# Twelve of the gate tiles of the first half computed in six pairs, seven products for eight, with PSUM banks read in the middle of their sums

## The chip, the cores and the metric

The kernel runs on one core of a Trainium2 chip. The metric is device time in microseconds (us), the median of three runs. Engines are named as the profile names them: PE is TensorE, PEld its weight loads, DVE is VectorE, ACT is ScalarE, POOL is GpSimd, and SP is SyncE, which here issues every DMA, one after the other in the order of its queue.

## The reference

One layer of a decoder on a sequence of 2048 tokens (and 16 meta tokens ahead of them), 1024 features wide, in float32. All projections come from one matrix of 1024 x 6400:

```python
xn = rms_norm(h, norm_gain[l])
proj = xn @ w_in[l]
sb_q, sb_k, sb_v, sw_q, sw_k, sw_v, sb_z, sw_z, g_sb, g_sw = jnp.split(proj, offsets, axis=-1)
o_sb = stick_breaking_attention(sb_q, sb_k, sb_v, valid)            # 8 heads, full length
o_sw = sliding_window_sink_attention(rope(sw_q), rope(sw_k), sw_v)  # 16 heads, window 128
y_sb = (o_sb * jax.nn.silu(sb_z)) @ w_branch_sb[l]
y_sw = (o_sw * jax.nn.silu(sw_z)) @ w_branch_swa[l]
merged = jax.nn.sigmoid(g_sb) * y_sb + jax.nn.sigmoid(g_sw) * y_sw
h = h + merged @ w_out[l]
return rms_norm(h, final_norm_gain)
```

(Reshapes and masks are left out.) The last four parts of the projection, `sb_z` (512 columns), `sw_z`, `g_sb` and `g_sw` (1024 each), are the gates: 28 tiles of 128 columns. They need nothing of the attention, so the kernel can compute them at any point where TensorE has room.

## The kernel before

**Tiles.** The sequence is cut into four groups of 512 columns. Groups 2 and 3 are the first half and are worked through from the projection to the two attentions; groups 0 and 1 are the second half. Features lie on the partitions, in eight slices of 128 (`k`). To keep float32 accuracy each matrix is split into a high and a low part of a type that TensorE multiplies at full rate (fp32r), and a product of such matrices is three matmuls: high by high, high by low, low by high. One tile of the projection (128 columns of `w_in` against one group) is therefore 8 x 3 = 24 matmuls into one PSUM bank, written by `gemm` (lines 409, 410, 411). A gate tile is done by `gate`: 24 matmuls for each of the two groups of the half, a sigmoid on ACT that reads the bank (L577), for `sw_z` and `sb_z` a multiplication on DVE (L579), and a store of 256 KB to DRAM.

**Weights.** `weights` serves one column tile. In the first half it loads the raw 512 KB into one of two `raw` buffers, splits it (`wh` by a copy, L108, `wl` by a subtraction, L109; on POOL while the flags `hsplit` and `vsplit` are False, on ACT and DVE when they are True), and stores both parts to DRAM. In the second half it loads the two stored parts (two times 512 KB). `wh` and `wl` have three buffers each.

**The stick-breaking attention** (`stick`) runs in rows: a product of keys and queries (L876), a sigmoid on ACT (L879), for the diagonal blocks a mask on POOL (L881), a scan along the row on DVE (L883), four transposes on PE (L896), the split of their result on ACT (L112) and DVE (L113), and the product with the values (L927). TensorE works on a row's transposes some five rows after its L876 (`LT`). The first half has 96 rows, 64 of them with the mask; the second has 224. DVE is the busiest of the engines that a row needs, so `weave` puts the k steps of gate tiles between the rows, at a ratio that spreads the rows over the gate tiles given to it: tiles 4 to 24 in the first half (`rest = 25`), 4 to 22 in the second. Tiles 0 to 3 come earlier. In the first half a row also carries, in 16 of the cases, the squares of the input of the second half (`xq`, L860), whose sums the normalization of that half needs; `xq` shares two buffers with the queries `q`.

**Between the halves.** After the last row of the first half, three gate tiles are left. `by_group` computes all three for group 2 and the first for group 3; then `prep` normalizes and splits the input of group 0 into the buffers of group 2 (a row `rb` from ACT, L374; then for each of eight slices a load `xs`, L382 on DVE, L383 on ACT, L385 on DVE), while TensorE does the two gate tiles left for group 3.

**Order.** The order on TensorE is written out by hand; that of DVE, ACT, POOL and SP in this part is set by the scheduler of the program from its estimates, and each engine works strictly in the order given to it.

## Time and profile before

| what | value |
|---|---|
| median of three runs | 2133.44 us (2133.14 to 2135.09) |
| profiled execution: time, span | 2136.89 us, 2135.0 us |
| PE busy, matmul records | 2112.2 us, 10534 |
| DVE, ACT, POOL busy | 1383.4, 1030.5, 333.1 us |
| DMA moved | 380.39 MB, 178 GB/s over the span |
| stretch of the stick-breaking rows, first half | about 395 to 738 us |
| the same, second half | about 1138 to 1627 us |

A row of the timeline gives start, duration, engine, line, operation, output and inputs, and in brackets how long the engine stood idle before it and what released it. Matmuls overlap, so the time that one costs is the distance between starts and not its duration. Of a table by stretches the columns are the busy time of PE, PEld, DVE, ACT and POOL with the count of instructions, then the granted clock, the share of the DMA engines and GB/s.

### The profile page before, as it was taken

The numbers are of one execution on the slowest core, as the hardware profiler recorded it, in microseconds if no ns is written. First come the engines' busy times: TensorE is split into PE (matmuls) and PEld (weight loads), VectorE is DVE, ScalarE is ACT, GpSimd is POOL, SyncE is SP. The second block draws the span as 40 slices with busy tenths as digits, with TensorE's granted clock in tenths as the row PEclk, the third lists the DMA queues.
The fourth block names the chain that finished last, engine by engine and source line by source line (L and its number), as shares of the span: only waits on it lengthen the run. The fifth ranks groups of instructions, "written<-read, shape, count | busy, mean of one in ns | idle before, by whom it ended". The sixth has DMA issues, their size and how long they took to land.

```text
span 2135.0 us, 30157 instructions
## 1 busy us (share of the span) xinstructions
PE 2112.2 (99%) x10534; PEld 1755.9 (82%) x10534; DVE 1383.4 (65%) x2158; ACT 1030.5 (48%) x2471; POOL 333.1 (16%) x453
## 2 busy tenths in 40 slices
PE   8999999999999999999999999999999999999998
PEld 6788888888888788888888888888888888887887
DVE  7797885466555443867746888888885446553453
ACT  6677774344444434777744565555554202221121
POOL 2122332332232300122210000000000232000000
PEclk9999999999999999999999999999999999999999
DMA  9855455766556464443465333323423986557432
GB/s 334 289 182 194 173 177 175 233 219 208 183 184 204 151 221 159 157 157 139 138 196 165 121 123 118 120 97 112 119 85 132 346 297 198 192 216 270 157 110 79
DMA packets 174519, 380.39 MB, mean 178 GB/s; under 512 B 22720, under 2 KB 40960, under 8 KB 174368
## 3 DMA queue, kind: packets, MB, share of 16 engines
q1 hardware_dynamic: 174368, 378.48, 52.5%
q8 instruction: 83, 1.36, 0.3%
q14 instruction: 68, 0.56, 0.1%
HBM read 237.35 MB, written 140.98 MB: 177 GB/s over the span
## 4 chain that ended last, share of the span: by engine, by line
PE 85%; issue 7%; DMA 3%; DVE 2%; ACT 1%; SPq 1%; POOL 0%; POOLq 0%; DVEq 0%; ACTq 0%
PE ps_g L409 15%; PE ps_g L411 14%; PE ps_g L410 14%; PE ps_o L927 5%; PE ps_t L896 4%; PE ps_z L876 4%; PE ps_z L718 3%; PE ps_o L764 3%; PE ps_g L232 1%; PE ps_g L233 1%; PE ps_z L231 1%; PE ps_z L233 1%; PE ps_z L232 1%; PE ps_g L231 1%; PE ps_t L747 1%
## 5 line engine op out<-in xcount | busy, mean ns | idle before, releaser
L409 PE MATMUL ps_g<-xh,wh 128*128 128x512 f32 x1544 | 634.6, 411 | 7.0 <-ACT xh L979 7.0
L410 PE MATMUL ps_g<-xl,wh 128*128 128x512 f32 x1544 | 605.9, 392 | 0.0
L411 PE MATMUL ps_g<-xh,wl 128*128 128x512 f32 x1544 | 605.9, 392 | 0.0
L883 DVE TENSOR_TENSOR_SCAN row<-row 128x512 f32<-128x512 f32 (+2 forms) x320 | 375.6, 1175 | 157.9 <-POOL row L881 105.8
L411 PEld LDWEIGHTS ps_g<-xh,wl 128*128 128x128 f32 x1544 | 290.2, 188 | 65.5 <-DVE wl L109 0.3
L409 PEld LDWEIGHTS ps_g<-xh,wh 128*128 128x128 f32 x1544 | 291.3, 189 | 52.7 <-ACT xh L979 7.0
L410 PEld LDWEIGHTS ps_g<-xl,wh 128*128 128x128 f32 x1544 | 292.0, 189 | 43.2 <-DVE xl L980 1.3
L879 ACT ACTIVATE row<-ps_z 128x512 f32<-128x512 f32 (+2 forms) x320 | 165.0, 516 | 192.0 <-PE ps_z L876 191.3
L113 DVE SCALAR_TENSOR_TENSOR wtl<-ps_t,wth 128x512 fp32r<-128x512 f32 (+1 forms) x320 | 189.9, 594 | 55.7 <-ACT wth L112 54.9
L112 ACT ACTIVATE wth<-ps_t 128x512 fp32r<-128x512 f32 (+1 forms) x320 | 170.5, 533 | 71.8 <-PE ps_t L896 68.9
L876 PE MATMUL ps_z<-kt,q 128*128 128x512 f32 (+4 forms) x640 | 178.2, 353 | 0.0
L896 PE MATMUL ps_t<-ident,row 128*128 128x128 f32 x1088 | 171.1, 272 | 1.9 <-DVE wtl L113 1.2
L896 PEld LDWEIGHTS ps_t<-ident,row 128*128 128x128 f32 x1088 | 135.7, 140 | 39.1 <-DVE wtl L113 2.3
L881 POOL TENSOR_SCALAR_AFFINE_SELECT row<-row 128x128 f32<-128x128 f32 x128 | 42.0, 329 | 630.1 <-ACT row L879 591.0
L876 PEld LDWEIGHTS ps_z<-kt,q 128*128 128x128 f32 x640 | 118.9, 188 | 23.2
L927 PE MATMUL ps_o<-wth,vc 128*128 128x512 f32 (+1 forms) x320 | 125.1, 391 | 0.0
L108 POOL TENSOR_SCALAR wh<-raw 128x1024 fp32r<-128x1024 f32 (+1 forms) x63 | 68.2, 1082 | 336.1 <-PE ps_g L410 209.5
L726 ACT ACTIVATE sc<-sc,nm 128x129 f32<-128x129 f32 x256 | 100.2, 394 | 41.7 <-DVE nm L724 40.9
L927 PE MATMUL ps_o<-wtl,vc 128*128 128x512 f32 (+1 forms) x320 | 116.9, 365 | 0.7 <-DVE wtl L113 0.7
L577 ACT ACTIVATE tmp<-ps_g 128x512 f32<-128x512 f32 x112 | 67.0, 599 | 103.9 <-PE ps_g L411 97.5
L109 POOL TENSOR_TENSOR wl<-raw,wh 128x1024 fp32r<-128x1024 f32 (+1 forms) x43 | 100.5, 2337 | 3.3
L270 ACT CAST ringl<-gt 128x512 fp32r<-128x512 f32 x32 | 20.0, 624 | 152.3 <-DVE gt L268 144.6
(316 smaller groups left out, 3439.2 us busy)
## 6 DMA issues: line engine op xcount, KB each, us to landing
wh<-h_in_w_in SPq DMA_DIRECT2D x66, 512.0 KB, 3.6
wl<-l_in_w_in SPq DMA_DIRECT2D x66, 512.0 KB, 4.9
raw<-in_w_in SPq DMA_DIRECT2D x50, 512.0 KB, 5.1
h_in_w_in<-wh SPq DMA_DIRECT2D x50, 512.0 KB, 2.9
l_in_w_in<-wl SPq DMA_DIRECT2D x50, 512.0 KB, 2.9
q<-qd SPq DMA_DIRECT2D x128, 128.0 KB, 3.1
vc<-vd SPq DMA_DIRECT2D x48, 256.0 KB, 3.3
kd<-tmp SPq DMA_DIRECT2D x32, 256.0 KB, 3.9
```

What stands on the lines that cost most here:

```text
L109: (V if vsplit[0] else G).tensor_tensor(l, src, f32(h), op=ALU.subtract)
L112: A.activation(h, acc, AF.Copy, scale=scale)
L113: V.scalar_tensor_tensor(l, acc, scale, f32(h), op0=ALU.mult, op1=ALU.subtract)
L409: T.matmul(acc, lhsT=wh[:, k, :], rhs=xh[g][:, k, :], start=k == 0, stop=False)
L410: T.matmul(acc, lhsT=wh[:, k, :], rhs=xl[g][:, k, :], start=False, stop=False)
L411: T.matmul(acc, lhsT=wl[:, k, :], rhs=xh[g][:, k, :], start=False, stop=k == KT - 1)
L726: A.activation(sc[:, hh, :], sc[:, hh, :], AF.Exp, bias=nm[:, hh:hh + 1], accum_out=den[:, hh:hh + 1])
L876: T.matmul(acc[:, :b - a], lhsT=lq, rhs=kt[h][:, k0 + a:k0 + b], start=t == 0, stop=t == 1)
L879: A.activation(r[:, a:b], acc[:, :b - a], AF.Sigmoid, scale=-1.0)
L883: V.tensor_tensor_scan(r[:, :w], r[:, :w], r[:, :w], last[j] if n else 1.0, op0=ALU.mult, op1=ALU.min)
L896: T.transpose(tr[:, j * P:(j + 1) * P], rows_of[h, g, n - (j > i), j][:, k0:k0 + P], ident)
L927: T.matmul(o[:, :n], lhsT=v, rhs=r, start=first and r is wh, stop=last and r is wl)
```

## The change

Gate tiles are regrouped. The list of 28 is now `sb_z` (4), `g_sb` (8), four of `g_sw`, `sw_z` (8), the other four of `g_sw`. In the first half only tiles 4 to 11 (the eight of `g_sb`) are woven into the stick-breaking rows (`REST[0] = 12`; the ratio goes from 0.60 to 1.58, the second half's stays 1.515). After the rows come three tiles of `g_sw` (12, 13, 14) the usual way, their weights split on ACT and DVE, and then tiles 16 to 27 as six pairs. Tile 15 is computed for group 2 ahead of `prep` and for group 3 behind it.

A pair is a product of a 2 x 2 block matrix of weights (two column tiles by two halves of the features) with a 2 x 2 block matrix of inputs (two halves of the features by two groups). It is done in Winograd's form of Strassen's scheme: seven block products of 4 x 3 = 12 matmuls each, 84 for a pair where two tiles for two groups took 96. The blocks are sums of blocks. `sums_of_x` makes those of the input once, in four steps of 12 DVE operations and four ACT copies; the first three steps stand ahead of the three usual tiles on the other engines, as far as the scheduler leaves them there. `pair_weights` makes those of the weights for each pair: it loads two raw tiles into the two `raw` buffers, and DVE and ACT form sums and high and low parts. `seven` does the products in three PSUM banks: two banks are read when a part of their sum is in and are then added to further (`start=False`). Since `KEEP_PAIRS` is False, the split weights of these twelve tiles are not stored; in the second half `weights` finds no stored parts for them and loads the raw tile, splits it on POOL, and stores the parts, which nobody reads. Seven of those tiles lie among the woven ones of the second half, five behind them.

```diff
+REST = (12, 23)
+KEEP_PAIRS = False
...
+    def sums_of_x(bp, groups):
...
+        for k in range(KT // 2):
+            yield q
+            b11, b12, b22 = (whole(n, k) for n in ("11", "12", "22"))
+            V.tensor_tensor(b11, b12, b11, op=ALU.subtract)
+            V.tensor_tensor(b12, b22, b12, op=ALU.subtract)
+            V.tensor_tensor(b22, b22, b11, op=ALU.subtract)
+            halves_of("t2", k, b22)
+            halves_of("t3", k, b12)
+            halves_of("t1", k, b11)
+            b21 = whole("21", k)
+            V.tensor_tensor(b21, b21, b22, op=ALU.subtract)
+            halves_of("t4", k, b21)
+        yield q
+
+    def pair_weights(bp, ca, cb):
...
+            a, b = load(ca), load(cb)
...
+            def parts(hl, t):
+                A.copy(hl[0], t)
+                V.tensor_tensor(hl[1], t, f32(hl[0]), op=ALU.subtract)
+            parts(t1, a)
+            V.tensor_tensor(s[:, hi], a[:, lo], b[:, lo], op=ALU.subtract)
+            V.tensor_tensor(b[:, lo], b[:, lo], b[:, hi], op=ALU.add)
+            V.tensor_tensor(s[:, lo], b[:, lo], a[:, lo], op=ALU.subtract)
+            parts(t3, s)
+            parts(t2, b)
+            V.tensor_tensor(s4, a[:, hi], s[:, lo], op=ALU.subtract)
+            parts(t4, s4)
...
+    def seven(w, b, tags, use):
...
+        a0, a1, a2 = (ps(t) for t in tags)
+        p1, u2, u3 = tmp(), tmp(), tmp()
+        product(a0, "11", "11", True, False)
+        A.copy(p1, a0)
+        product(a1, "s2", "t2", True, False)
+        V.tensor_tensor(u2, a1, p1, op=ALU.add)
+        product(a0, "12", "21", False, True)
+        use(0, 0, a0)
+        product(a1, "s3", "t3", False, False)
+        V.tensor_tensor(u3, a1, p1, op=ALU.add)
+        product(a2, "s1", "t1", True, False)
+        V.tensor_tensor(u3, a2, u3, op=ALU.add)
+        use(1, 1, u3)
+        product(a1, "22", "t4", False, True)
+        V.tensor_tensor(p1, a1, p1, op=ALU.add)
+        use(1, 0, p1)
+        product(a2, "s4", "22", False, True)
+        V.tensor_tensor(u2, a2, u2, op=ALU.add)
+        use(0, 1, u2)
...
-            rest = 25 if half == 0 else 23
+            rest = REST[half]
...
-            ts = [mk() for mk in gts[rest:]]
-            drain(by_group(ts, groups[:1]), by_group(ts[:1], groups[1:]))
+            with tc.tile_pool(name="pairs", bufs=1, side="left") as bp:
+                hsplit[0] = vsplit[0] = True
+                ts = [mk() for mk in gts[rest:15]]
+                hsplit[0] = vsplit[0] = False
+                sums_q = sums_of_x(bp, groups)
+                tq = [next(sums_q) for _ in range(3)][0]
+                for n, t in enumerate(ts):
+                    if n == 1:
+                        next(sums_q)
+                    drain(by_group([t], groups))
+                pairs = [gate_pair(bp, gss[n], gss[n + 1], groups, tq) for n in range(16, 28, 2)]
+                next(pairs[0])
+                next(sums_q)
+                drain(*pairs)
+            ts = [gts[15]()]
+            drain(by_group(ts, groups[:1]))
             prep(halves[1][0], rs0)
-            drain(by_group(ts[1:], groups[1:]))
+            drain(by_group(ts, groups[1:]))
```

Lines of the changed kernel stand two lower than before up to the new functions (L55 becomes L57, L579 becomes L581), and 114 lower behind them (L876 becomes L990). In the rows below a name's number is that of the tile, and the brackets name the engines or DMA queues whose semaphores the instruction waits for.

**The hand-over to the pairs, on DVE.** Before, the last split of the rows (`wtl`) and the reciprocal root for the next half's normalization are followed at once by `prep`:

```order
L113 SCALAR_TENSOR_TENSOR wtl_8261<-ps_t_8255,wth_8260 128x512 [waits Activation_49]
L117 TENSOR_SCALAR sum_8279<-sum_8279 128x8 [waits DVE_49]
L932 TENSOR_TENSOR xs_7610<-tmp_8274 64x512 [waits Activation_49]
L123 TENSOR_TENSOR sum_8280<-rs_8283 128x8 [waits DVE_49,PE_49,Activation_49]
L934 TENSOR_TENSOR xs_7610<-tmp_8270,xs_7610 128x512
L124 TENSOR_TENSOR sum_8280<-sum_8280,sum_8279 128x8 [waits DVE_49]
L125 TENSOR_SCALAR sum_8280<-sum_8280 128x8 [waits DVE_49]
L126 TENSOR_TENSOR rs_8283<-rs_8283,sum_8280 128x8 [waits DVE_49]
L382 SCALAR_TENSOR_TENSOR xs_8443<-xs_8443,gn_67,rb_8436 128x512 [waits DMAHW3_49,Activation_49]
L382 SCALAR_TENSOR_TENSOR xs_8448<-xs_8448,gn_67,rb_8436 128x512 [waits DMAHW7_49,DMAHW0_49]
```

Now the sums of the input and of the weights of the first pairs stand in between. Below is the stretch about the last of them: `wl_7692` is the low part of the sum t2 of pair 0, `t3l`, `t2l` are slices of the input sums, and `s_7857<-raw_7853,raw_7855` (L636) is the first sum of pair 1, whose raw tiles are loaded at that point.

```order
L634 TENSOR_TENSOR wl_7692<-raw_7697,wh_7691 128x1024 [waits DMAHW5_49,PE_49,Activation_49]
L634 TENSOR_TENSOR s4l_7694<-tmp_7700,s4h_7693 128x512 [waits Activation_49]
L606 TENSOR_TENSOR tmp_7713<-tmp_7715,tmp_7713 128x512 [waits DVE_49]
L607 TENSOR_TENSOR tmp_7715<-tmp_7717,tmp_7715 128x512 [waits DVE_49]
L601 TENSOR_TENSOR t1l_7456<-tmp_7713,t1h_7455 128x512 [waits Activation_49]
L608 TENSOR_TENSOR tmp_7717<-tmp_7717,tmp_7713 128x512 [waits DVE_49]
L636 TENSOR_TENSOR s_7857<-raw_7853,raw_7855 128x512 [waits DMAHW6_49,DMAHW0_49]
L601 TENSOR_TENSOR t3l_7454<-tmp_7715,t3h_7453 128x512 [waits Activation_49]
L613 TENSOR_TENSOR tmp_7728<-tmp_7728,tmp_7717 128x512 [waits DVE_49]
L637 TENSOR_TENSOR raw_7855<-raw_7855 128x512 [waits DVE_49]
L601 TENSOR_TENSOR t2l_7452<-tmp_7717,t2h_7451 128x512 [waits Activation_49]
```

The last slices of `t3l` and `t2l`, which pair 0 reads, stand behind L636 of pair 1 on the same engine.

**In a pair, on DVE and SP.** Before, the leftover tiles need nothing of DVE, and SP carries their stores and, from row `wh_8542` on, the loads for the next half:

```order
L55 DMA gw5_2_229<-tmp_8347 128x512 [waits DMAHW4_49,Activation_49]
L55 DMA gw6_2_233<-tmp_8375 128x512 [waits DMAHW5_49,Activation_49]
L55 DMA gw7_2_237<-tmp_8403 128x512 [waits Activation_49]
L55 DMA wh_8542<-h_in_w_in_512_318 128x1024 [waits DMAHW7_49,PE_49]
L55 DMA wl_8543<-l_in_w_in_512_319 128x1024 [waits DMAHW0_49,PE_49]
L55 DMA gw5_3_230<-tmp_8431 128x512 [waits DMAHW1_49,Activation_49]
```

Now DVE does this about the boundary of pairs 0 and 1 (L680 is the last addition for pair 0, L641 its neighbour for the weights s4 of pair 1, L636 and L637 are the first sums of pair 2, and L668 reads pair 1's bank z when its second product is in):

```order
L680 TENSOR_TENSOR tmp_7737<-ps_t_7735,tmp_7737 128x512 [waits PE_49]
L641 TENSOR_TENSOR tmp_7858<-raw_7853,s_7857 128x512 [waits DMAHW1_49]
L691 TENSOR_TENSOR tmp_7841<-tmp_7737,tmp_7841 128x512 [waits Activation_49]
L634 TENSOR_TENSOR s4l_7852<-tmp_7858,s4h_7851 128x512 [waits Activation_49]
L636 TENSOR_TENSOR s_7995<-raw_7991,raw_7993 128x512 [waits DMAHW5_49,DMAHW3_49]
L637 TENSOR_TENSOR raw_7993<-raw_7993 128x512 [waits DVE_49]
L668 TENSOR_TENSOR tmp_7875<-ps_z_7872,tmp_7874 128x512 [waits DMAHW2_49,PE_49,Activation_49]
L638 TENSOR_TENSOR s_7995<-raw_7993,raw_7991 128x512 [waits DVE_49]
```

and SP this (`raw_7991` and `raw_7993` are the tiles of pair 2, into the buffers of `raw_7853` and `raw_7855`):

```order
L57 DMA zw0_2_145<-tmp_7777 128x512 [waits DMAHW1_49,DVE_49]
L57 DMA zw1_3_150<-tmp_7807 128x512 [waits DMAHW2_49,DVE_49]
L57 DMA raw_7991<-in_w_in 128x1024 [waits DMAHW3_49,DMAHW0_49,DVE_49]
L57 DMA zw1_2_149<-tmp_7824 128x512 [waits DMAHW4_49,DVE_49]
L57 DMA raw_7993<-in_w_in 128x1024 [waits DMAHW6_49,DMAHW5_49,DVE_49]
L57 DMA zw0_3_146<-tmp_7841 128x512 [waits DVE_49]
```

L668 of pair 1, which TensorE needs before it adds its fourth product to that bank, stands behind the sums of pair 2 and so behind their loads.

**`prep` of group 0, on ACT.** Before, one gate tile's sigmoid (`tmp_8431`) ends ahead of `rb`, and two more (`tmp_8508`, `tmp_8536`) run between the copies of the input slices:

```order
L577 ACTIVATE tmp_8431<-ps_g_8406 128x512 [waits DMAHW1_49,PE_49]
L374 COPY rb_8436<-ps_t_8437 128x512 [waits PE_49]
L383 CAST xh_8434<-xs_8443 128x512 [waits DVE_49]
L383 CAST xh_8434<-xs_8448 128x512 [waits DVE_49]
L383 CAST xh_8434<-xs_8453 128x512 [waits DVE_49]
L383 CAST xh_8434<-xs_8458 128x512 [waits DVE_49]
L577 ACTIVATE tmp_8508<-ps_g_8483 128x512 [waits DMAHW2_49,PE_49]
L383 CAST xh_8434<-xs_8463 128x512 [waits DVE_49]
L383 CAST xh_8434<-xs_8468 128x512 [waits DVE_49]
L383 CAST xh_8434<-xs_8473 128x512 [waits DVE_49]
L577 ACTIVATE tmp_8536<-ps_g_8511 128x512 [waits PE_49,Activation_49]
L383 CAST xh_8434<-xs_8478 128x512 [waits DVE_49]
```

Now it is the only tile's sigmoid for group 3 (`tmp_8634`) that stands between the fourth and the fifth copy, and the next copies are followed by the second half's own:

```order
L579 ACTIVATE tmp_8557<-ps_g_8532 128x512 [waits DMAHW3_49,PE_49,Activation_49]
L376 COPY rb_8562<-ps_t_8563 128x512 [waits PE_49]
L385 CAST xh_8560<-xs_8569 128x512 [waits DVE_49]
L385 CAST xh_8560<-xs_8574 128x512 [waits DVE_49]
L385 CAST xh_8560<-xs_8579 128x512 [waits DVE_49]
L385 CAST xh_8560<-xs_8584 128x512 [waits DVE_49]
L579 ACTIVATE tmp_8634<-ps_g_8609 128x512 [waits DMAHW4_49,PE_49,Activation_49]
L385 CAST xh_8560<-xs_8589 128x512 [waits DVE_49]
L385 CAST xh_8560<-xs_8594 128x512 [waits DVE_49]
L385 CAST xh_8560<-xs_8599 128x512 [waits DVE_49]
L385 CAST xh_8560<-xs_8604 128x512 [waits DVE_49]
```

TensorE has one tile for one group to do behind `rb` there, where before it had two.

61 lines of the change are left out of this document (57 added, 4 removed).

## The prediction

> **What bounds the kernel now.** I read the page first, then a table by stretches, then the waits of TensorE, then the timeline at the places that the change touches.
>
> ```profile
> span 2135.0 us, 30157 instructions
> PE 2112.2 (99%) x10534; PEld 1755.9 (82%) x10534; DVE 1383.4 (65%) x2158; ACT 1030.5 (48%) x2471; POOL 333.1 (16%) x453
> PE 85%; issue 7%; DMA 3%; DVE 2%; ACT 1%; SPq 1%; POOL 0%; POOLq 0%; DVEq 0%; ACTq 0%
> ```
>
> PE is busy for 99% of the span and carries the chain that ends last. So a matmul removed is time gained, unless PE then waits. PE's waits are few now:
>
> ```profile
> PE ps_g L409 <- ACT xh L979: 7.0, 1, 7.0
> PE ps_o L409 <- ACT xh L383: 1.6, 1, 1.6
> PE ps_t L896 <- DVE wtl L113: 1.2, 2, 0.6
> ```
>
> None of these lies at the leftover gate tiles or at `prep` of group 0 (there PE runs on, below). Every new wait is therefore a loss that the kernel does not have now.
>
> ```profile
> 500.00:600.00 100.00, 99.34 (x513) 82.61 (x512) 55.52 (x69) 45.78 (x114) 25.95 (x28) 1.00 0.59 194
> 1300.00:1400.00 100.00, 100.00 (x545) 83.73 (x544) 83.65 (x103) 58.53 (x125) 3.54 (x12) 1.00 0.40 121
> 1700.00:1800.00 100.00, 100.00 (x443) 82.84 (x442) 48.48 (x58) 11.43 (x19) 32.66 (x24) 1.00 0.74 263
> ```
>
> The first row is the woven stretch of the first half: DVE (third pair of columns) 56%, POOL 26%. The second is that of the second half: DVE 84%, and POOL nearly idle, since weights come split; the third, the tail of the second half, is spoken of at the end. The change makes the first stretch as dense as the second, and puts POOL's splits into both.
>
> **What is gained.** Matmuls follow each other at 0.228 us:
>
> ```profile
> 695.11 0.39 PE L409 MATMUL ps_g<-xh,wh 128*128 128x512 f32 x1
> 695.33 0.39 PE L410 MATMUL ps_g<-xl,wh 128*128 128x512 f32 x1
> 695.56 0.40 PE L411 MATMUL ps_g<-xh,wl 128*128 128x512 f32 x1
> ```
>
> Between the starts at 738.25 and 760.03 (both rows below) stand 96, so 0.227 each over whole tiles. Six pairs save 12 matmuls each, 72 in all: 72 x 0.227 = 16.3 us. A product of 12 takes 2.72 us, a pair 19.1 instead of 21.8, a tile for one group (24) 5.45. The other matmuls only move. Now the waits.
>
> **(a) The hand-over into the pairs.** Call T0 the end of the rows:
>
> ```profile
> 738.25 0.39 PE L409 MATMUL ps_g<-xh,wh 128*128 128x512 f32 x1
> ```
>
> Three usual tiles hold PE until T0 + 6 x 5.45 = 32.7. DVE is free of the square root at about T0 + 4 and does 36 operations of the input sums ahead of the pairs. What 512 columns cost:
>
> ```profile
> 1651.92 0.69 DVE L199 TENSOR_TENSOR tmp<-tmp 128x512 f32<-128x512 f32 x1 [0.66 <-DMA tmp<-zw]
> 1652.53 0.68 DVE L203 TENSOR_TENSOR ringl<-tmp,ringl 128x512 fp32r<-128x512 f32 x1
> ```
>
> 0.61 us start to start, so 22 us: hidden under the three tiles. But the third weight sum of pair 0 takes the `wh` and `wl` buffers of the third tile, which PE frees at T0 + 32.7. Then:
>
> ```profile
> L109 DVE TENSOR_TENSOR wl<-raw,wh x22: 1205/1220/1627, 14.3 to 345.7; 128x1024 fp32r<-128x1024 f32 x22
> L106 ACT CAST wh<-raw x2: 1032/1043/1054, 13.2 to 15.4; 128x1024 fp32r<-128x1024 f32 x2
> DMA to landing us min/median/max: 4.2/5.1/8.8
> ```
>
> The cast on ACT (1.04) and the subtraction on DVE (1.22) end at T0 + 35.2; only then is the raw buffer free, and SP issues the second raw tile of pair 1 at about T0 + 35.6. The last row is the landing of raw tiles in the whole trace; 8.8 belongs to the first 50 us, and the one measured in each later stretch took
>
> ```profile
> DMA to landing us min/median/max: 4.2/4.2/4.2
> DMA to landing us min/median/max: 5.1/5.1/5.1
> ```
>
> from 50 to 395 and from 395 to 740 us. On DVE the sum L636 of pair 1 waits for that tile, and the last slices of pair 0's input sums stand behind it: five operations, 3.1 us. They end at T0 + 42.9 to 43.8, and PE asks for the last slice of t2 in its second product, at T0 + 32.7 + 2.72 + 2.04 = 37.5. Wait 5.4 to 6.3, taken 5.8. Without the load DVE's own queue (ten operations) ends at T0 + 41.3, wait 3.8; with 8.8 it is 10.0. After a wait of that size PE may start slowly; the one long wait of the trace ends so:
>
> ```profile
> 7.01 0.79 PE L409 MATMUL ps_g<-xh,wh 128*128 128x512 f32 x1 [7.01 <-ACT xh L979]
> 8.81 0.63 PE L409 MATMUL ps_g<-xh,wh 128*128 128x512 f32 x1
> 11.64 0.39 PE L409 MATMUL ps_g<-xh,wh 128*128 128x512 f32 x1
> ```
>
> Nine matmuls in 4.63 us, 2.6 more than at 0.227, partly for want of input. I take half, 1.3 (0 to 2.6). The Trainium skill, "TensorE: Matmul & The Clock Gate", section "Part 1: The HAM clock gate", has TensorE fall to half its clock when it idled for a window of some 3.4 us, until it was busy about as long again; by that rule the term would be about 1.7 (an estimate from that page). **(a) = 7.1**, 3.8 to 12.6.
>
> **(b) Between pairs.** The raw tiles of pair n+2 can be loaded when DVE has done s4 of pair n+1, behind the last addition of pair n. DVE's read of bank z (L668) in pair n+1 stands behind the two sums of pair n+2, which wait for these loads; PE's fourth product may not start before that read. From the end of pair n: 0.17 release, two operations 0.61 + 0.69, issues 0.85, landing 4.6 (between the two rows above), two sums and the read 2.0: 8.9. PE arrives after three products, 8.2. Late by 0.7, in four of the six pairs: **(b) = 2.8**; at 4.2 us of landing 1.3, at 5.1 it is 4.9, at 8.8 it would be 19.7. The reads in the middle cost no more than this: the copy of the first bank on ACT (0.6 us, as a sigmoid of that shape below) has the second product, 2.72 us, to hide behind; if that cover went, the third product would be late.
>
> **(c) `prep` of group 0.** PE needs the last low slice for the eighth step of the first product of the second half:
>
> ```profile
> 760.03 0.60 PE L368 MATMUL ps_t<-ident,rs 128*128 128x128 f32 x4
> 771.75 0.48 PE L409 MATMUL ps_g<-xh,wh 128*128 128x512 f32 x1
> 776.64 0.39 PE L409 MATMUL ps_g<-xh,wh 128*128 128x512 f32 x1
> ```
>
> ```profile
> 761.34 2.74 DVE L382 SCALAR_TENSOR_TENSOR xs<-xs,gn,rb 128x512 f32<-128x512 f32 x4 [18.91 <-ACT rb L374]
> 771.70 1.41 DVE L382 SCALAR_TENSOR_TENSOR xs<-xs,gn,rb 128x512 f32<-128x512 f32 x2 [1.36 <-DMA xs<-in_xt]
> 774.14 0.69 DVE L385 TENSOR_TENSOR xl<-xs,xh 128x512 fp32r<-128x512 f32 x1 [0.31 <-ACT xh L383]
> ```
>
> Now the slice is there at 774.8 and asked for (L410) at 776.9: 2.1 us to spare. One tile less of cover, 5.5 us, makes it 3.4 late at this pace; without the waits for loads (eight of each at 0.70 and 0.68, 11.0 us from 761.3) it is there at 772.4, 1.0 late. The last two loads again stand behind a weight load on SP, so I stay near the first: **(c) = 2.8**.
>
> **(d) The woven stretches.** Fifteen splits on POOL fall into dense stretches, eight in the first half, seven in the second, where before loads of split weights stood. What one does to DVE:
>
> ```profile
> 507.39 2.32 DVE L883 TENSOR_TENSOR_SCAN row<-row 128x272 f32<-128x272 f32 x1 [0.28 <-ACT row L879]
> 520.49 0.72 DVE L883 TENSOR_TENSOR_SCAN row<-row 128x272 f32<-128x272 f32 x1 [1.34 <-POOL row L881]
> ```
>
> ```profile
> 506.74 2.39 POOL L109 TENSOR_TENSOR wl<-raw,wh 128x1024 fp32r<-128x1024 f32 x1
> ```
>
> The same scan takes 2.32 us instead of 0.72 beside POOL's subtraction, and ends with it. The Trainium skill ("SBUF — State Buffer", section "Who interferes with whom") calls the port pair that DVE shares with GpSimd an exclusive lock; these rows agree. Scans came 3.4 us apart so far, and PE hardly noticed:
>
> ```profile
> L883 DVE TENSOR_TENSOR_SCAN row<-row x96: 448/1224/3319, 398.4 to 724.2; 128x512 f32<-128x512 f32 x32, 128x528 f32<-128x528 f32 x16, 128x400 f32<-128x400 f32 x16, 128x272 f32<-128x272 f32 x16
> ```
>
> With 13 tiles of 10.9 us taken out they come about 2 us apart, as in the second half. There the room is this:
>
> ```profile
> 1301.86 0.60 PE L896 MATMUL ps_t<-ident,row 128*128 128x128 f32 x4
> 1305.52 0.60 PE L896 MATMUL ps_t<-ident,row 128*128 128x128 f32 x4
> ```
>
> ```profile
> 1303.21 0.67 DVE L113 SCALAR_TENSOR_TENSOR wtl<-ps_t,wth 128x512 fp32r<-128x512 f32 x1
> ```
>
> The bank t of the first transposes is read out at 1303.88 and taken again at 1305.52: 1.64 us to spare. A delay of 1.60 just fits; the longest that the trace has,
>
> ```profile
> 1667.85 2.88 DVE L203 TENSOR_TENSOR ringl<-tmp,ringl 128x512 fp32r<-128x512 f32 x1
> ```
>
> against 0.68, with some 0.4 before it, is 2.6, so 1.0 over. Between 0 and 1.0 for each split, I take 0.2, nearer the scan's row since it is the scan that fills DVE there: 15 x 0.2 = 3.0 (0 to 15; a gain is excluded, PE is at 100% there). Next, the squares share buffers with the queries:
>
> ```profile
> DMA to landing us min/median/max: 3.2/4.1/5.0
> DMA to landing us min/median/max: 2.6/3.1/4.8
> L577 ACT ACTIVATE tmp<-ps_g 128x512 f32<-128x512 f32 x112 | 67.0, 599 | 103.9 <-PE ps_g L411 97.5
> ```
>
> `xq` lands in 4.1, is squared in about 0.8, and then `q` in 3.1: 8.0 us, against four rows and their gate steps, about 9.7 (53 matmuls at 0.183, 545 in 100 us). At the upper ends it is 10.6. I take 0.2 for each of seven heads, 1.4 (0 to 7). At the end of the rows a tile's split on DVE (1.22) stands ahead of the last `wtl`: half, 0.6. **(d) = 5.0.**
>
> **Costed at nothing.** In the tail of the second half, five splits on POOL and stores that nobody reads: DVE is at 48% there, POOL has a row of weights ahead of PE, and the stores wait on SP only for POOL. Should POOL be late, the first gate tile of the tail is.
>
> **The sum.** 7.1 + 2.8 + 2.8 + 5.0 = 17.7 lost against 16.3 gained: +1.4 us. The profiled execution (2136.89, span 2135.0) would go to 2138.3; it lies 3.45 above the median 2133.44, so the median goes to **2134.8**, with its own range 2130 to 2139.
>
> **Rivals.** *Loads and splits are covered (faster).* DMA moves little while pairs run (two raw tiles and four stores in 19 us), so landing is at the low end, 4.2 or less, and DVE does not stop PE in the rows. For it: the 84% of DVE in the second half leave PE at 100%. Against: the order on DVE. (a) 3.8, (b) 1.3, (c) 1.5, (d) 0.6: 7.2 lost, 9.1 gained, 2124. *POOL's lock stops the rows (slower).* Place: L113 in both dense stretches, 15 splits. Price: 1.0 each instead of 0.2, +12, so 2147. For it: 2.88 us beside POOL, and masks of the first half queue on POOL behind a split of 3.4 us. Against: DVE idles 16 us in 100 and catches up before the next split, some 25 us later. It decides from 0.4 us for each split. *Raw tiles take 7 us in the pairs (slower).* 2.4 more than taken in four pairs and in (a): +12, 2147; spoken for only by the first 50 us.
>
> **How the numbers follow.** A measurement tells about 0.2% from no change, 4.3 us. Forecast 0.40, covered loads 0.30, lock 0.22, slow loads 0.08. The forecast's range reaches a little over both bounds of 4.3, so faster 0.31, same 0.38, slower 0.31. The range takes in both rivals' centres: 2123 to 2147.
>
> **What would show it.** PE with 72 matmuls less; a wait of some 5.8 us on `t2l` in the first pair; four of under 1 us on L668; one of 2 to 3 us at the first tile of the second half; waits on L113 in the rows that lie just behind a POOL subtraction. The forecast is wrong if the pairs run at 19.1 us each without waits, or if the waits on L113 sum to over 6 us.

## The result: 33 us slower, and where they went

The changed kernel takes 2166.41 us (median of four runs, 2164.77 to 2166.51), the kernel before 2133.29 in the same comparison: ratio 1.0152, 95% interval 1.0135 to 1.017. The prediction was 2134.8 (2123 to 2147). From the page of the changed kernel:

```profile
span 2164.6 us, 30201 instructions
PE 2112.2 (98%) x10462; PEld 1748.4 (81%) x10462; DVE 1466.1 (68%) x2287; ACT 1057.8 (49%) x2520; POOL 328.5 (15%) x447
PE 60%; DVE 4%; DMA 4%; issue 2%; ACT 1%; SPq 0%; POOL 0%; DVEq 0%; POOLq 0%; ACTq 0%
```

72 matmuls are gone, but PE's busy time is the same 2112.2 us, and the span is 29.6 longer. (By the medians it is 33.1; the profiled execution of the kernel before, 2136.89, lies 3.6 above its median.) The list of PE's waits, here down to 1.2 us, shows one part (columns: total us, times, longest); that of before had 7.0, 1.9, 1.6 and 1.2 at its head, the 7.0 being the same wait at the start.

```profile
PE ps_t L1010 <- DVE wtl L115: 9.1, 13, 1.5
PE ps_g L411 <- ACT xh L1093: 7.0, 1, 7.0
PE ps_g L411 <- ACT tmp L579: 5.8, 2, 5.0
PE ps_g L233 <- ACT tmp L579: 5.2, 1, 5.2
PE ps_t L1010 <- DVE wm L115: 3.5, 6, 1.3
PE ps_z L661 <- DVE t2l L601: 2.5, 1, 2.5
PE ps_g L411 <- ACT xh L385: 2.2, 1, 2.2
PE ps_o L1041 <- ACT tmp L1045: 2.0, 3, 1.0
PE ps_g L234 <- DVE ringl L205: 1.9, 2, 1.4
PE ps_z L661 <- DVE tmp L668: 1.7, 4, 0.6
PE ps_z L661 <- ACT t2h L600: 1.2, 1, 1.2
```

The other part is the clock behind a wait. Matmuls that otherwise start 0.227 us apart start about 0.43 us apart there, and the table by stretches shows a granted clock of 0.50 to 0.66 (PE busy with its count first, granted clock third from the end):

```profile
623.00:627.00 4.00, 4.00 (x10) 3.13 (x11) 4.00 (x7) 1.84 (x4) 0.00 (x0) 0.50 0.35 131
653.00:660.00 7.00, 4.24 (x10) 3.16 (x11) 5.00 (x8) 0.83 (x2) 0.00 (x0) 0.66 0.00 0
791.50:795.50 4.00, 4.00 (x12) 3.16 (x12) 3.18 (x5) 2.10 (x4) 0.00 (x0) 0.57 0.81 271
1716.00:1720.00 4.00, 3.88 (x9) 3.15 (x10) 2.53 (x5) 2.89 (x4) 0.00 (x0) 0.50 0.84 278
```

To see all of it, I cut both timelines of PE at the same seven instructions and compared the stretches; "matmuls" is the change of their number by 0.227 us each, "lost" the rest.

| stretch on PE | before | after | matmuls | lost |
|---|---|---|---|---|
| to the first product of the rows | 395.2 | 393.6 | 0 | -1.6 |
| rows, first half | 343.0 | 213.1 | -141.6 | 11.7 |
| usual tiles and pairs, to `rb` of `prep` | 21.8 | 170.0 | +130.8 | 17.4 |
| to the second `rb` | 11.4 | 5.9 | -5.5 | 0 |
| to the first row of the second half | 366.8 | 372.0 | 0 | 5.2 |
| rows, second half | 495.1 | 500.2 | 0 | 5.1 |
| tail, to the first branch product (L233) | 54.8 | 61.2 | 0 | 6.4 |
| the rest | 439.3 | 441.1 | 0 | 1.8 |
| sum | 2127.4 | 2157.1 | -16.3 | 46.0 |

Of the 17.4, 7.7 lie ahead of the first pair (40.4 us for six products of a tile with a group, not 32.7), 7.0 in pair 0, and 0.5, 0.7, 0.6 and 0.9 in the next four. The sum of 46.0, less the 16.3 gained, is the 29.7 by which the two profiled timelines differ. Five places on the timeline:

**Ahead of the pairs.** ACT's queue, and PE behind it:

```profile
618.63 0.62 ACT L600 CAST t1h<-tmp 128x512 fp32r<-128x512 f32 x1 [1.79 <-DVE tmp L606]
619.76 1.04 ACT L633 CAST wh<-raw 128x1024 fp32r<-128x1024 f32 x1
620.82 1.28 ACT L579 ACT_TABLE_LOAD   x1
622.11 0.60 ACT L579 ACTIVATE tmp<-ps_g 128x512 f32<-128x512 f32 x1
```

```profile
622.76 0.79 PE L411 MATMUL ps_g<-xh,wh 128*128 128x512 f32 x1 [4.98 <-ACT tmp L579]
```

(One more cast of 0.62 us, at 619.23, is left out.) The sigmoid of the first usual product, whose matmuls ended at about 612, stands on ACT behind casts of the input sums, which wait for DVE, and behind a cast of weights and a table load. There are two banks g, so the third product waits for that sigmoid.

**Pair 0.** DVE and then PE:

```profile
648.15 1.22 DVE L634 TENSOR_TENSOR wl<-raw,wh 128x1024 fp32r<-128x1024 f32 x1 [4.24 <-ACT wh L633]
653.10 0.69 DVE L636 TENSOR_TENSOR s<-raw 128x512 f32<-128x512 f32 x1 [0.54 <-DMA raw<-in_w_in]
655.51 0.69 DVE L601 TENSOR_TENSOR t2l<-tmp,t2h 128x512 fp32r<-128x512 f32 x1
```

```profile
656.25 0.80 PE L661 MATMUL ps_z<-t2l,wh 128*128 128x512 f32 x1 [2.49 <-DVE t2l L601]
701.55 0.50 PE L661 MATMUL ps_z<-t3h,wh 128*128 128x512 f32 x1 [0.41 <-DVE tmp L668]
```

This is the chain of the prediction's (a), in its order, and in the last row its (b). The load of pair 1's raw tile held DVE for only 0.54 us; the rest is DVE's own queue behind the weight split. By the starts of PE's rows the last slice of t2 came 4.2 us late (as idle time, which counts from the end of the matmul before, 1.25 for its high part and 2.49 for its low part), and the 14 matmuls from there on took 6.0 us instead of 3.2.

**A row of the first half.** ACT, DVE, PE:

```profile
424.99 0.64 ACT L974 ACTIVATE xq<-xq 128x512 f32<-128x512 f32 x1 [2.94 <-DMA xq<-in_x]
425.62 0.58 ACT L993 ACTIVATE row<-ps_z 128x512 f32<-128x512 f32 x1
```

```profile
426.60 1.23 DVE L997 TENSOR_TENSOR_SCAN row<-row 128x512 f32<-128x512 f32 x1 [2.82 <-POOL row L995]
428.46 0.44 PE L1010 MATMUL ps_t<-ident,row 128*128 128x128 f32 x2 [1.47 <-DVE wtl L115]
```

ACT stands before a square whose load has not landed, with a row's sigmoid behind it; the mask on POOL, the scan on DVE and at last the transposes follow late.

**A row of the second half.** POOL, DVE, PE:

```profile
1412.43 2.71 POOL L111 TENSOR_TENSOR wl<-raw,wh 128x1024 fp32r<-128x1024 f32 x1
1412.91 2.78 DVE L1048 TENSOR_TENSOR xs<-tmp,xs 128x512 f32<-128x512 f32 x1
1417.26 0.66 PE L1010 MATMUL ps_t<-ident,row 128*128 128x128 f32 x4 [1.28 <-DVE wtl L115]
```

An operation of DVE that takes 0.68 us elsewhere takes 2.78 beside POOL's subtraction, and the transposes wait. PE waits for L115 six times in these rows, 5.5 us in all; five of the six, 4.9 us, lie beside a subtraction on POOL or less than 5 us behind one; ten such subtractions fall into this stretch. In the first half most of these waits lie further from one: the 1.47 us above come 10 us after the last.

**The tail.** SP, POOL, DVE, ACT, PE:

```profile
1708.50 0.39 SPq L57 DMA_DIRECT2D tmp<-zw  x1
1711.95 2.34 POOL L111 TENSOR_TENSOR wl<-raw,wh 128x1024 fp32r<-128x1024 f32 x1
1712.44 2.39 DVE L201 TENSOR_TENSOR tmp<-tmp 128x512 f32<-128x512 f32 x1 [4.04 <-DMA tmp<-zw]
1714.86 0.62 ACT L203 CAST ringl<-tmp 128x512 fp32r<-128x512 f32 x1 [5.81 <-DVE tmp L201]
1716.12 0.77 PE L233 MATMUL ps_g<-ringl,wh 128*128 128x512 f32 x1 [5.17 <-ACT tmp L579]
```

DVE waits 4.04 us for a load that SP issued at 1708.50, and its operation of 0.69 us then takes 2.39 beside POOL's subtraction; ACT's sigmoid (1715.39) stands behind a cast that waits for both.

### The profile page after: what moved, and what is told of

It reads as the page before. It is cut to its first block, busy times and chain, and to the rows that moved or that the text cites. A ratio compares the mean times of both kernels' runs of the same rounds, so it can differ in the third digit from the quotient of the medians.

```text
span 2164.6 us, 30201 instructions
## 1 busy us (share of the span) xinstructions
PE 2112.2 (98%) x10462; PEld 1748.4 (81%) x10462; DVE 1466.1 (68%) x2287; ACT 1057.8 (49%) x2520; POOL 328.5 (15%) x447
## 4 chain that ended last, share of the span: by engine, by line
PE 60%; DVE 4%; DMA 4%; issue 2%; ACT 1%; SPq 0%; POOL 0%; DVEq 0%; POOLq 0%; ACTq 0%
PE ps_g L411 7%; PE ps_g L412 7%; PE ps_g L413 7%; PE ps_o L1041 4%; PE ps_t L1010 4%; PE ps_z L990 4%; PE ps_z L661 2%; PE ps_t L661 2%; PE ps_g L234 1%; PE ps_z L832 1%; PE ps_g L235 1%; PE ps_g L233 1%; PE ps_z L233 1%; PE ps_z L234 1%; PE ps_z L235 1%
## 5 line engine op out<-in xcount | busy, mean ns | idle before, releaser
L411 PE MATMUL ps_g<-xh,wh 128*128 128x512 f32 x1352 | 556.5, 412 | 15.3 <-ACT xh L1093 7.0
L412 PE MATMUL ps_g<-xl,wh 128*128 128x512 f32 x1352 | 533.0, 394 | 0.4 <-DVE xl L387 0.2
L413 PE MATMUL ps_g<-xh,wl 128*128 128x512 f32 x1352 | 532.5, 394 | 0.0
L411 PEld LDWEIGHTS ps_g<-xh,wh 128*128 128x128 f32 x1352 | 256.8, 190 | 58.2 <-ACT xh L1093 7.0
L413 PEld LDWEIGHTS ps_g<-xh,wl 128*128 128x128 f32 x1352 | 255.4, 189 | 56.9
L412 PEld LDWEIGHTS ps_g<-xl,wh 128*128 128x128 f32 x1352 | 257.0, 190 | 41.7 <-DVE xl L387 1.4
L115 DVE SCALAR_TENSOR_TENSOR wtl<-ps_t,wth 128x512 fp32r<-128x512 f32 (+1 forms) x320 | 188.9, 591 | 26.5 <-ACT wth L114 25.7
L990 PE MATMUL ps_z<-kt,q 128*128 128x512 f32 (+4 forms) x640 | 179.2, 355 | 0.1
L1010 PEld LDWEIGHTS ps_t<-ident,row 128*128 128x128 f32 x1088 | 133.4, 140 | 53.2 <-DVE wtl L115 17.7
L990 PEld LDWEIGHTS ps_z<-kt,q 128*128 128x128 f32 x640 | 117.3, 188 | 21.2 <-ACT row L993 0.5
L1041 PE MATMUL ps_o<-wth,vc 128*128 128x512 f32 (+1 forms) x320 | 129.8, 406 | 2.1 <-ACT tmp L1045 2.0
L995 POOL TENSOR_SCALAR_AFFINE_SELECT row<-row 128x128 f32<-128x128 f32 x128 | 49.5, 389 | 507.4 <-ACT row L993 462.4
L579 ACT ACTIVATE tmp<-ps_g 128x512 f32<-128x512 f32 x88 | 52.4, 597 | 89.2 <-PE ps_g L413 81.9
L111 POOL TENSOR_TENSOR wl<-raw,wh 128x1024 fp32r<-128x1024 f32 (+1 forms) x40 | 93.4, 2334 | 3.0
```

The costliest lines, as they stand in the source:

```text
L111: (V if vsplit[0] else G).tensor_tensor(l, src, f32(h), op=ALU.subtract)
L115: V.scalar_tensor_tensor(l, acc, scale, f32(h), op0=ALU.mult, op1=ALU.subtract)
L411: T.matmul(acc, lhsT=wh[:, k, :], rhs=xh[g][:, k, :], start=k == 0, stop=False)
L412: T.matmul(acc, lhsT=wh[:, k, :], rhs=xl[g][:, k, :], start=False, stop=False)
L413: T.matmul(acc, lhsT=wl[:, k, :], rhs=xh[g][:, k, :], start=False, stop=k == KT - 1)
L990: T.matmul(acc[:, :b - a], lhsT=lq, rhs=kt[h][:, k0 + a:k0 + b], start=t == 0, stop=t == 1)
```

## The experiments

All start from the changed kernel unless it is said otherwise. Stretches in us as above; "left" runs from the end of the rows to `rb`. The rows of the first half of the changed code took 212.8 to 216.0 us where an edit didn't touch them, so a difference of 3 there says nothing. The stretch between the two `rb` is not in the table: it took 5.9 us with one product of a tile with a group, and 11.4 with two in g3_combined, h1_order, h2_keep_a and the two k runs. In the first three of these a product of 5.5 us has moved there out of "left".

| run | total | rows 1 | left | to row of half 2 | rows 2 | tail | rest |
|---|---|---|---|---|---|---|---|
| changed kernel | 2166.4 | 213.1 | 170.0 | 372.0 | 500.2 | 61.2 | 441.1 |
| e1_eight | 2155.6 | 216.0 | 168.7 | 373.2 | 494.8 | 54.8 | 439.0 |
| e2_kept | 2173.2 | 212.8 | 188.0 | 372.6 | 494.8 | 54.8 | 438.9 |
| e3_act_split | 2167.8 | 216.7 | 170.1 | 372.3 | 500.2 | 60.8 | 441.2 |
| e4_banks | 2158.8 | 215.6 | 162.2 | 374.3 | 500.2 | 59.5 | 442.7 |
| f1_no_xq | 2162.5 | 210.0 | 170.0 | 372.9 | 500.1 | 61.0 | 440.6 |
| f2_pool_copy | 2166.0 | 216.9 | 170.8 | 371.8 | 500.2 | 59.1 | 439.5 |
| f3_lent | 2172.2 | 218.8 | 168.5 | 371.8 | 504.2 | 58.6 | 438.8 |
| f4_second | 2187.9 | 213.3 | 169.2 | 401.8 | 500.3 | 54.8 | 437.4 |
| g1_no_mask | 2165.3 | 215.0 | 170.8 | 372.1 | 500.2 | 59.1 | 439.0 |
| g2_four_pairs | 2172.5 | 257.7 | 133.9 | 373.2 | 496.9 | 61.9 | 441.0 |
| g3_combined | 2148.3 | 213.2 | 161.7 | 366.6 | 500.1 | 54.8 | 437.5 |
| g4_lag7 | 2169.0 | 215.4 | 170.8 | 373.9 | 499.5 | 58.5 | 441.5 |
| h1_order | 2146.5 | 212.1 | 157.9 | 366.7 | 500.0 | 54.8 | 439.5 |
| h2_keep_a | 2143.0 | 214.6 | 159.0 | 366.7 | 497.0 | 55.6 | 437.3 |
| h3_no_hops | 2152.5 | 203.8 | 170.1 | 370.5 | 500.1 | 59.6 | 439.6 |
| k1_five | 2135.5 | 214.5 | 152.6 | 366.8 | 496.0 | 58.2 | 439.4 |
| k2_five_pool | 2133.1 | 209.5 | 153.1 | 366.6 | 496.3 | 54.8 | 439.3 |

Totals are medians for the e runs (two each), h1_order (3), h2_keep_a (5), k1_five and k2_five_pool (11 each), and one run for the others.

**e1_eight**, the grouping alone:

```diff
-                sums_q = sums_of_x(bp, groups)
...
-                drain(*pairs)
+                drain(tiles_by_tile(gts[16:28], groups))
```

> The changed kernel with its grouping (8 tiles woven into the rows of the first half, tile 15 around prep), but tiles 16 to 27 computed with all eight products, their weights split on POOL and stored; no sums of the input. Theory A (what the two traces show by stretches: rows of the first half 11.8 us too long, leftover tiles 7.7, pairs 9.8, prep 5.2, rows of the second half 5.1, tail 8.3, against 16.3 gained): the rows of the first half stay about 12 too long and prep about 5, and all the rest is gone, so about 2133 + 12 + 5 - 2 = 2148. Theory B (the pairs and their sums are the whole cause, and the first-half rows suffer from the other order only by way of them): 2133 to 2137.

2155.55, ratio 1.0103 (1.0073 to 1.0132): 7.5 us above the 2148 of theory A, and far above theory B. The loss lies where theory A has it. Rows of the first half and `prep` lose as much as in the changed kernel or a little more, and the second half is as before. So the grouping alone costs 22 us; the changed kernel loses 33 after a gain of 16, that is 49, and so the grouping is somewhat under half of what it loses. The stretch with the pairs, 72 matmuls shorter, took 170.0 us where the same stretch with all eight products took 168.7.

**e2_kept**, all parts stored:

```diff
...
+            kl = [tmp(F32R).rearrange("p (k c) -> p k c", k=KT // 2) for _ in "hl"]
+            parts(kl, b[:, lo])
+            for c, pieces in ((ca, [(slice(0, KT), t1)]), (cb, [(lo, kl), (hi, [t[:, hi] for t in t2])])):
+                ks = kept[w_in.name, c] = [dram(f"{t}_{w_in.name}_{c}", [P, KT, P], F32R) for t in "hl"]
+                keeps.append((ks, pieces))
...
+            for ks, pieces in keeps:
+                for r, ts in pieces:
+                    for k, t in zip(ks, ts):
+                        DMA(k[:, r], t)
```

> The changed kernel, with the split parts of the twelve pair tiles stored in the first half (one more split of 512 columns and 2 MB of stores for each pair), so that the second half loads them as before. Theory A: the rows of the second half (5.1 us too long) and the tail (8.3) come back to before: 2166 - 13 = 2153, less 1 to 4 us that the added split and stores cost in the pairs. Theory B: the second half suffers from the regrouping or from contention of another kind, and the added stores only cost: 2166 to 2172.

The second half came back to before in all three stretches (494.8, 54.8, 438.9): its 13.3 us are due to the raw tiles. The pairs paid 18, where 1 to 4 were expected. PE waits for ACT's cast of a weight sum; that cast waits for the sum on DVE (L644), which stands behind the added split (`tmp<-raw,tmp`):

```profile
PE ps_z L671 <- ACT wh L634: 12.8, 5, 3.0
```

```profile
674.04 0.68 DVE L635 TENSOR_TENSOR tmp<-raw,tmp 128x512 fp32r<-128x512 f32 x1
675.49 0.69 DVE L644 TENSOR_TENSOR s<-raw 128x512 f32<-128x512 f32 x1
677.36 0.50 PE L671 MATMUL ps_z<-t2h,wh 128*128 128x512 f32 x1 [2.69 <-ACT wh L634]
```

**e3_act_split** and **f3_lent**, POOL's splits taken out of the rows:

```diff
+        if asplit[0]:
+            A.copy(h, src)
+            A.copy(l, src)
+            return
...
+            asplit[0] = half == 0
```

> The changed kernel, with the eight tiles woven into the rows of the first half split by two copies on ACT (the low part is a copy instead of a difference, so the gates g_sb are wrong in value), so that POOL has only masks there and DVE nothing more. Theory A (POOL's subtraction locks DVE and stands ahead of the masks): the rows of the first half, 11.8 us too long, come to under 4 too long, total about 2157. Theory B (the rows are too dense for their chain of engines, whoever splits): 9 us or more too long stay, total 2163 to 2168.

```diff
+        if key in kept or lend[0]:
+            for t, k in zip((wh, wl), kept[w.name, C_SBZ] if lend[0] else kept[key]):
...
+            lend[0] = half == 0
```

> The changed kernel; the eight tiles woven into the rows of the first half load the stored split parts of an earlier tile (as the second half does), so they are neither split nor stored, and the values of g_sb are those of another tile. The splits are then gone from every engine. Theory of the prediction (POOL's splits, by their lock on DVE and ahead of the masks, are what stops dense rows): the rows of the first half come to 203 or less. Theories C and D: they stay at 208 or more.

216.7 and 218.8. Without any split on any engine PE still waits for `wtl`:

```profile
PE ps_t L1012 <- DVE wtl L115: 8.6, 10, 2.6
```

The splits are not what stops the rows of the first half. So POOL's lock on DVE falls for these rows, as the prediction's term and as its rival. No run took the splits off POOL in the rows of the second half.

**e4_banks**, the usual tiles in banks g, z, t:

```diff
-                    drain(by_group([t], groups))
+                    for g in groups:
+                        drain(lagged(col_tile(t[0], g, t[1], bank="gzt"[n])))
```

> The changed kernel, with the three usual tiles behind the rows in banks g, z and t instead of g alone, so that the third product does not wait for the sigmoid of the first (5.0 us, and a slow clock behind it). Theory A: the 7.7 us of that place go and the first pair is as late as now, total about 2159. Theory B: DVE and ACT with the sums are the limit there, so that what is gained ahead of the pairs comes back as a longer wait in the first pair: 2164 to 2167.

The stretch fell by 7.8 and pair 0 took 25.5 us, where the changed kernel has 26.1: theory A. The two runs were 2153.2 and 2164.45, too far apart for the total; the stretch is the measure.

**f1_no_xq, f2_pool_copy, g1_no_mask, g4_lag7**, one hop of the rows at a time:

```diff
-                    t = bp.tile([P, GT], F32, tag="q2", name="xq", bufs=2)
-                    DMA(t, x[g1 * GT + i * P:g1 * GT + (i + 1) * P, f * GT:(f + 1) * GT])
-                    A.activation(t, t, AF.Square, accum_out=ssq[:, f, i:i + 1])
+                    t = tmp()
+                    A.activation(t, f32(xh[groups[0]][:, 0, :]), AF.Square, accum_out=ssq[:, f, i:i + 1])
```

> The changed kernel; the 16 squares that ride on the rows of the first half read a tile that lies in SBUF instead of a loaded one (the loads are left out, and the sums, so the second half's scale, are those of other data). ACT's work stays. Theory C (ACT stands at the square until its load lands, 13.5 us in eleven waits in the rows, with the sigmoids and splits of the rows queued behind it): the rows of the first half, 213 to 216 us now against 201 at the cost of their matmuls, come to 206 or less. Theory D (the rows wait for each other through the copies of their last 16 columns on ACT, which wait for DVE's scan, 33.7 us in 45 waits): they stay at 211 or more.

```diff
-                A.copy(pair(h, g)[0][:, j, h % 2], r[:, w - NM:w])
+                G.tensor_scalar(pair(h, g)[0][:, j, h % 2], r[:, w - NM:w], 1.0, 1.0, op0=ALU.mult, op1=ALU.mult)
```

> The changed kernel, with the copy of the last 16 columns of the 64 end rows of each half on POOL instead of ACT. Theory C: the rows of the first half stay at 211 us or more. Theory D: they come to 206 or less, since ACT no longer stands behind DVE's scan. The rows of the second half stay at 500.

```diff
-            if n == 0:
+            if n == 0 and groups[0] == 0:
```

> The changed kernel without the masks on POOL in the 64 diagonal rows of the first half (those rows then let later keys in, so the values are others). DVE waits 20.1 us for a mask in the rows of the first half, 29 times. Theory E (the extra step over POOL in two thirds of the rows makes the chain of a dense row too long): the rows of the first half, 213 to 217 us, come to 206 or less. Theory F (what is left of the loss is density alone, 2.2 us a row for all engines): they stay at 210 or more.

```diff
-LT = 5
+LT = 7
```

> The changed kernel with the transposes seven rows behind the keys' product instead of five, in both halves. If the rows of the first half are stopped by delays of single rows that a longer lag absorbs, they come from 213 to 217 down to 206 or less, those of the second half from 500 to 497; if DVE's and ACT's work in their order is the limit, they stay at 211 or more.

210.0, 216.9, 215.0, 215.4, of one run each. The square's load is worth 3 to 6 us, which fits neither theory C (206 or less) nor D (211 or more); the others alone show nothing. In f2_pool_copy ACT no longer waited for the scans, but 19.3 us instead of 14.2 before the squares: the wait that was taken out came back in part at another.

**h3_no_hops**, three at once:

> The changed kernel with three things taken out of the rows of the first half at once that alone left 210, 217 and 215 us: the squares' loads, the end rows' copies on ACT (now on POOL), the masks (left out). If the loss of 12 us is the sum of such short waits in line, the rows come to 204 or less; if it is the change of heads (transposes of the meta part, the one bank o, 16 in 213 us), they stay at 208 or more.

203.8: 9.3 of the 11.7 us are gone. PE's largest wait in these rows:

```profile
PE ps_t L1009 <- DVE wtl L115: 2.8, 4, 1.4
```

So most of the loss comes from short waits in line, which together are worth more than taken out one by one (3 to 6, 0 and 0). A count of the gaps on PE, by the starts of its rows against the usual distance for each shape and from 0.3 us on, gives about 12 us in 17 places of these rows for the changed kernel, about 6 in 10 for h3_no_hops and 2 in 3 before: by this count half of it stays.

**g2_four_pairs**, rows less dense:

```diff
-REST = (12, 23)
+REST = (16, 23)
```

> Twelve tiles woven instead of eight, then three usual ones, four pairs, and one tile around prep. The rows get 2.55 us each. At the cost of their matmuls they take 201.3 + 43.6 = 244.9 us. If density is what stops them, their loss of 12 to 15 us falls to 4 or less (249); if it is a fixed cost of squares and masks, it stays above 9 (254). The gain of the products is 10.9 instead of 16.3, the second half has eight raw tiles instead of twelve. Total 2150 to 2155 in the first case, 2160 in the second.

257.7, 12.8 above 244.9: the loss did not shrink at 2.7 us a row, and the total, 2172.5, lies 12 above the 2160 of that case. A fixed cost of squares and masks, as the expectation had it, is not the whole answer either: before has the same squares and masks at 3.6 us a row, and its loss there is the zero of this count. Where between 3.6 and 2.7 the loss sets in was not looked for.

**f4_second**, stores and splits of the second half's tail:

```diff
+        if second[0] and w is w_in:
+            return wh, wl
...
+            second[0] = half == 1
...
+            hsplit[0] = vsplit[0] = True
             for mk in gts[rest:]:
```

> The changed kernel; in the second half the parts of tiles that nobody reads again are not stored, and in the tail the five tiles are split on ACT and DVE instead of POOL. If the stores in SP's order and POOL's lock made the tail late, the tail comes from 61 to 55 us, and the stretch behind it from 441 to 439; the rows of the second half keep their 5 us, since POOL still splits seven tiles there. If the loads of raw tiles are the cause, the tail stays at 60 or more.

The edit did more than that: its switch has the name of a list used earlier in the program, so tiles of the first half were not stored either, and 24 tiles were loaded raw and split behind `prep`, where the changed kernel has 2 (401.8 instead of 372.0; the total tells nothing). Its tail answers: 54.8 and 437.4, with the rows at 500.3. Stores and splits were taken away together, so their shares stay open.

**g3_combined**, the mended switch, banks, and the last usual tile's group 3 behind `prep`:

```diff
+            hsplit[0] = vsplit[0] = True
             for mk in gts[rest:]:
...
-            ts = [gts[15]()]
-            drain(by_group(ts, groups[:1]))
+            ts = [gts[15](), gts[14]()]
+            drain(by_group(ts[:1], groups[:1]))
             prep(halves[1][0], rs0)
```

> The changed kernel with three of its losses taken away: the usual tiles in banks g, z, t; the last of them done for group 3 behind prep, as cover; in the second half no stores that nobody reads, and the tail's five tiles split on ACT and DVE. If the losses add up as the stretches say, 2166 - 7.8 - 5 - 8 = 2145, with prep's stretch at 367 to 368 and the tail at 55. If they only move, one of the next stretches grows: the first pair by up to 5 us (its sums have 5.4 us less cover), total 2150.

2148.26. `prep` (366.6) and tail (54.8) are as before the change. Pair 0 went from 26.1 to 30.2, since its sums had 5.4 us less cover: that loss only moved.

```profile
PE ps_z L665 <- ACT t2h L604: 5.8, 1, 5.8
```

**h1_order** and **h2_keep_a**:

```diff
-                    if n == 1:
+                    if n in (1, 2):
                         next(sums_q)
...
-                    t = bp.tile([P, GT], F32, tag="q2", name="xq", bufs=2)
+                    t = bp.tile([P, GT], F32, tag="xq", name="xq", bufs=2)
```

> As g3_combined, and two more edits, each in a stretch of its own. First, the last step of the input sums is issued ahead of pair 0's weights, so that it no longer stands on DVE behind the third weight sum (which waits for a buffer of PE) and the loads of pair 1. If that order is what makes pair 0 late, pair 0 takes 19.1 to 21 us instead of 30.2; if DVE and ACT have simply too much to do there, 26 or more. Second, the squares' loads have two buffers of their own and are issued a head ahead. If the square's load is what ACT waits for, the rows of the first half come from 213 to 210 or less, as without the loads (210.0); if not, they stay at 213 to 217. Total 2148 - 9 - 4 = 2135 if both hold.

Pair 0 took 27.3: order was 3 us of the 11 that it was late. The rest is the amount of work, for DVE has hardly a gap from shortly behind the rows into pair 0, which starts at 634.4 (37.90 us busy of 38.00, third pair of columns):

```profile
610.00:648.00 38.00, 32.39 (x136) 25.78 (x135) 37.90 (x62) 18.02 (x28) 0.00 (x0) 0.93 0.21 78
```

The rows came to 212.1, between the two cases. The first squares now waited ahead of the first rows, which cost PE 2.0 us of waiting and, at a granted clock of 0.75 from 400.2 to 407.0, some 1.7 more, so the edit to the squares is not answered by this run. The total is 11.5 above the 2135 for both edits.

```diff
+            kept[w_in.name, ca] = [dram(f"{t}_{w_in.name}_{ca}", [P, KT, P], F32R) for t in "hl"]
+            for k, t in zip(kept[w_in.name, ca], t1):
+                DMA(k, t)
...
+                gts[16:] = gts[16::2] + gts[17::2]
```

> As h1_order, and the split parts of the first tile of each pair (which are the sums' t1 anyway) are stored, 1 MB a pair; in the second half the six tiles so stored come first, so one raw tile is left in the rows and five in the tail. If the raw tiles are what costs 5 us in the rows of the second half, they come from 500 to 496; if storing is what stopped the pairs of e2_kept, half of its 18 us shows again in the pairs (23 us each instead of 19.7); if it was the buffers of t2 and t3 waiting for their stores there, the pairs stay at 20.

The second half's rows gained 3 (497.0), and the pairs stayed at 20: storing t1 is nearly free. So the 18 us of e2_kept lie in what it did to the second tile of a pair. Its trace points to the split that it added there (above), and shows no wait in pairs 1 to 5 for a store of weights; no run took the split or the stores alone.

**k1_five** and **k2_five_pool**, five pairs with four usual tiles ahead and two around `prep`, each square a head behind its load:

```diff
-                pairs = [gate_pair(bp, gss[n], gss[n + 1], groups, tq) for n in range(16, 28, 2)]
+                pairs = [gate_pair(bp, gss[n], gss[n + 1], groups, tq) for n in range(18, 28, 2)]
...
-            ts = [gts[15]()]
+            ts = [gts[16](), gts[17]()]
```

> Five pairs instead of six: four usual tiles ahead of them (43.6 us of cover for the sums instead of 27.2), two around prep as before the change, banks g, z, t in turn, sums issued early, parts of the first tile of each pair stored, no stores that nobody reads, raw tiles of the second half only in the tail, each square one head behind its load. Gain 60 matmuls, 13.6 us. If pair 0 was late by the amount of work on DVE (48 operations of 0.61 and the weights, some 37 us), it now takes 19.1 to 21 us; the rows of the first half 208 to 211 (still 7 to 10 too long), of the second 495. Total 2133.4 - 13.6 + 9 + 1 + 3 + 2 = 2134.8, between 2130 and 2138: the losses just about eat the gain.

> As k1_five, and the end rows' copies on POOL instead of ACT, in both halves. Alone that changed nothing (f2_pool_copy, 217); with squares and masks away the rows took 203.8. If short waits in line add up only once the square's wait is gone, the rows of the first half come 2 to 4 us below those of k1_five and the total 2131 to 2133; if the masks were the whole difference, nothing changes.

Pair 0 takes 19.0 us in both: with cover for the work the wait is gone. k1_five is 1.0009 of before (1.0000 to 1.0018), k2_five_pool 0.9994 (0.9985 to 1.0003). k1_five came out where its sum had it, with rows of the first half 3.5 to 6.5 us longer than expected there; its total is that of eleven runs, its stretches that of one. The rows' 5 us between the two are from one profile each, and k1_five's was its slowest run; the medians differ by 2.4. No version was clearly faster than before.

## Why the prediction was wrong, step by step

It had 17.7 us lost, and the stretches show 46.0, 28.3 more. Three steps failed: the size of (d), short by 11.8; the tail, put at nothing, 8.2; and the overlap "hidden under the three tiles", 7.7. The term (c) was short by 2.4, and the first stretch, which took 392 to 396 us over all runs, happened to take 1.6 less. Its own sign of being wrong came: the waits on L113, now L115, sum to 12.6 us, over 6.

- **The gain, 16.3**, held.
- **(b), 2.8**: measured 0.5 + 0.7 + 0.6 + 0.9 = 2.7, by the wait that was named, four times (1.7 us as idle time, 2.7 by the starts). The raw tiles of the pairs landed in 3.9 to 5.3 us, 4.6 in the median, as taken.
- **(a), 7.1**: pair 0 lost 7.0, but the agreement is luck: the slice came 4.2 us late instead of 5.8, since the load held DVE for 0.54 us only, and the slow clock behind it cost 2.8 instead of 1.3. And the step ahead of it, "so 22 us: hidden under the three tiles", failed: it looked at DVE's time alone. ACT's casts for these sums stand ahead of a sigmoid that frees a bank, and cost 7.7 there (5.0 of waiting, the rest the clock behind it). e4_banks took just these away. The chain of (a) was only a part of pair 0's cause: with its order mended, 8 of 11 us stayed (h1_order), and with 43.6 us of cover they went (k1_five). 48 operations and pair 0's own weights need more than the cover of 27.2 us there, or of 32.7 in the changed kernel.
- **(c), 2.8**: 5.2. The waits were 2.25 and 0.2, about as sized, one step of the product earlier than named; the slow clock behind them (0.57 in the table by stretches, from 791.5 to 795.5), some 1.6 us, was left out.
- **(d), 5.0**: 11.7 + 5.1 = 16.8, mis-sized and, for the first half, with the wrong cause. POOL's lock is real (2.78 us instead of 0.68 above) but was not what stopped those rows (e3_act_split, f3_lent); only six subtractions on POOL fell into them, not eight. The second half's 5 us do come from the raw tiles (e2_kept, h2_keep_a), and there the waits lie where the prediction put them, just behind POOL's subtractions: 4.9 us for ten, 0.5 each instead of 0.2. That it is the splits and not the loads is read from the trace, not tested. The square's load, priced at 1.4 for buffers shared with the queries, cost 3 to 6 by standing on ACT.
- **"Costed at nothing", the tail**: 8.2. The sentence "DVE is at 48% there" used an average; the chain SP, DMA, DVE, ACT, bank was tight, and f4_second and g3_combined brought it back by splits on ACT and DVE and without the stores, both at once.
- Of the rivals, "POOL's lock stops the rows" had the right side and nearly the size for (d): by the wrong mechanism in the first half, which is luck, and in the second by the right one as far as the trace shows. No single mechanism makes up the loss: the 46 us lie in seven places.

What stays open: how the 12 us of the first half's rows divide among squares, masks and copies (only their sum was shown), from which spacing of rows they begin, and what the split, the load and the store of a raw tile cost one by one in the second half.
